# Seven products of a block product summed in three PSUM chains, with partial sums copied out by ScalarE

## The chip, the cores and the metric

The kernel runs on one core of a Trainium2 chip. The metric is the device time of one execution in microseconds (us). A core has five engines, each with its own queue of instructions that it takes in order: TensorE (PE in the profile; its weight loads are PEld), VectorE (DVE), ScalarE (ACT), GpSimd (POOL) and SyncE (SP, which here only issues loads).

## What is computed

A decoder trunk of two layers on 512 tokens of width 1024, in float32. Layer 0 mixes tokens by attention, layer 1 by pooling; each is followed by a SwiGLU FFN of inner width 2816, and every part is preceded by an RMS norm.

```python
def swiglu_ffn(h, w_gate_up, w_down):
    gu = h @ w_gate_up
    gate, up = gu[..., :D_FF], gu[..., D_FF:]
    return (jax.nn.silu(gate) * up) @ w_down

def reference(x, attn_norm, w_qkv, ...):
    for i in range(DEPTH):
        j = i // N_MIXERS
        if i % N_MIXERS == 0:
            x = x + dilated_attention_mixer(rmsnorm(x, attn_norm[j]), w_qkv[j], w_attn_out[j])
        else:
            x = x + pooling_mixer(rmsnorm(x, pool_norm[j]), ...)
        x = x + swiglu_ffn(rmsnorm(x, ffn_norm[i]), w_ffn_gate_up[i], w_ffn_down[i])
    return rmsnorm(x, final_norm)
```

The attention has 8 heads in each of 3 groups; q, k and v of all of them come from one projection `h @ w_qkv`.

## The kernel before

**Split numbers.** Every operand of a large matmul is kept as two float32r tiles, a rounded value `hi` and the rest `lo` (`split`, lines 83 to 85: ScalarE makes `hi`, VectorE subtracts to get `lo`). A product of 128 contraction rows takes three matmuls: hi by hi, hi by lo, lo by hi.

**Block products.** Most of the q, k, v projections and 17 of the 22 column blocks of each FFN's gate and up projection are computed in pairs by the Winograd form of Strassen's scheme: two 128-column outputs (`one` and `two`, for instance gate and up) of 512 tokens from 1024 inputs, cut into quarters of 256 tokens, take seven products instead of eight. Each product (`mult`, lines 378 to 384) has 4 contraction steps by 3 matmuls on 128x256, so a block product has 84 matmuls. There are 55 of them through `seven` (lines 391 to 438): 21 in the attention stage, 34 in the FFN. Four more, for values of the other attention groups, go through `values12`. The first five column blocks of each FFN, the down projections and the pooling stage use plain products of 128x512 (`Product`, lines 262 to 265).

**Operands.** `normed` (lines 440 to 452) makes the sums and differences of token quarters that the scheme needs, and `prepare` (one for the attention, one for each FFN) splits them into the tiles `T["11"]`, `T["21"]`, `T["1"]` to `T["4"]`, `T["22"]`. The weights' sums are made per block product by a `Pair`: `blocks` splits the tile b, `sums` the tile s, `more` adds twice on VectorE (lines 158 and 159) and splits the tile m, `last` splits the half tile l. Products 1 and 2 use b, 5 and 7 use s, 6 and 3 use m, 4 uses l.

**Order of the work.** `seven` issues its products in the order 1, 2, 5, 7, 6, 3, 4, in four PSUM banks (p1, p26, p45, p73). Product 1 is copied out by ScalarE (line 410); VectorE does the other sums as the banks fill: line 423 (2 and 6 with 1), line 429 or 431 (7 and 3 with those), lines 436 and 437 (5 and 4 with those). After each product `behind(i)` calls `pump`, which issues at most one load and one step of the weights to come, as soon as a buffer of its ring is free (`BUFS`: five `w` tiles, two `half`, four `raw`); in the attention stage it also runs functions of the heads (`scores0`, `scores12`, `merge`, `turn0`, `turn12`, `output`), which use all engines. A weight tile is free when the last product that reads it has been issued and done. Loads go by SyncE's queue, and one addition per pair by an accumulating load on GpSimd's (line 145).

The instructions are then put on each engine's queue by the framework in the order in which they are expected to become ready; the written order decides between those that are ready.

In the FFN, `activation` (lines 896 and 897) follows each pair: Silu of the gate on ScalarE, the product with `up` on VectorE, and a split of the result.

Of the kernel before, what the change touches and what calls it, by code (L numbers as in the profile page):

```python
# [11 lines left out]
OP = mybir.AluOpType  # L12
# [43 lines left out]
def trunk(ctx: ExitStack, tc: tile.TileContext, xT, norms, w_first, w_qk, w_qkp, w_v0, w_v0p, w_v12, w_out, w_pair, w_down, w_pin, w_pgrp,  # L56
# [16 lines left out]
    def ps():  # L73
        return psum.tile([P, S], F32, tag="ps", name="ps")
# [8 lines left out]
    def split(hi, lo, v):  # L83
        nc.scalar.activation(hi, v, AF.Copy)  # L84
        nc.vector.tensor_tensor(lo, v, hi.bitcast(F32), op=OP.subtract)  # L85

    rings = {ring: [] for ring in BUFS}

# [286 lines left out]
    def in_place(t, a=slice(0, 2)):  # L375
        return t[:, a.start * H2:a.stop * H2]

    def mult(dst, w, half, T, name):
        for k in range(K2):
            c = slice(half * S + k * P, half * S + (k + 1) * P)  # L380
            th, tl = T[name, k]
            nc.tensor.matmul(dst, w.t[0][:, c], th, start=k == 0, stop=False)  # L382
            nc.tensor.matmul(dst, w.t[0][:, c], tl, start=False, stop=False)  # L383
            nc.tensor.matmul(dst, w.t[1][:, c], th, start=False, stop=k == K2 - 1)  # L384

    def part(unit, name):
        while name not in unit.w:
            pump(must=True)
        return unit.w[name]

    def seven(T, one, two, scratch, after={}, blocks=False):
# [5 lines left out]
        def again(v):  # L397
            return v.unsqueeze(1).to_broadcast([P, 2, H2])

        p1, p26, p45, p73 = ps(), ps(), ps(), ps()  # L400

        def behind(i):
            pump()
            for f in after.get(i, ()):
                f()

        w = part(unit, "b")
        mult(p1[:, :H2], w, 0, T, "11")
        first, sums = scratch("first"), scratch("sums")
        nc.scalar.copy(first[:, :H2], p1[:, :H2])  # L410
        behind(0)
        mult(p26[:, :H2], w, 1, T, "21")
        w.done()
        behind(1)
        w = part(unit, "s")
        mult(p45[:, H2:], w, 0, T, "1")
        behind(2)
        mult(p73[:, :H2], w, 1, T, "3")
        w.done()
        behind(3)  # L420
        w = part(unit, "m")
        mult(p26[:, H2:], w, 0, T, "2")
        nc.vector.tensor_add(into(one), p26, again(first[:, :H2]))
        behind(4)
        mult(p73[:, H2:], w, 1, T, "22")
        w.done()
        if blocks:
            for a in (left, right):
                nc.vector.tensor_add(in_place(sums, a), in_place(p73, a), into(one, right))
        else:  # L430
            nc.vector.tensor_add(sums, p73, again(one[:, H2:]))
        behind(5)
        w = part(unit, "l")
        mult(p45[:, :H2], w, 0, T, "4")
        w.done()
        nc.vector.tensor_sub(into(two), p45, again(sums[:, :H2]))
        nc.vector.tensor_sub(into(one, right), sums[:, H2:], p45[:, H2:])  # L437
        behind(6)

    def normed(layer, k, row):  # L440

        h, t = Held("raw"), Held("raw")
        for i in range(2):
            c = k + i * K2
            nc.vector.scalar_tensor_tensor(h.t[:, i * S:(i + 1) * S], X[c], nrm[:, layer, c:c + 1], row,  # L445
                                           op0=OP.mult, op1=OP.mult)
        hq = h.t.rearrange("p (a b c) -> p a b c", a=2, b=2)
        tq = t.t.rearrange("p (a b c) -> p a b c", a=2, b=2)
        nc.vector.tensor_sub(tq[:, :, 0], hq[:, :, 1], hq[:, 0])
        nc.vector.tensor_sub(t.t[:, H2:S], t.t[:, :H2], h.t[:, 3 * H2:])  # L450
        nc.vector.tensor_add(t.t[:, 3 * H2:], t.t[:, H2:S], h.t[:, S:3 * H2])
        return h, t

    def halves_of(hi, lo):
# [9 lines left out]
    with tc.tile_pool(name="opool", bufs=1) as opool:  # L464
        early = opool.tile([P, HEADS, S], F32R, tag="o", name="early")
        with tc.tile_pool(name="apool", bufs=1) as apool:
# [15 lines left out]
            def values12(after={}):  # L482


                t = apool.tile([P, NT, 4 * P], F32, name="v12")
                unit = units.popleft()

                def product(name, half, key):
                    p = ps()
                    for a in range(2):  # L490
                        for k in range(K2):
                            wh, wl = (v[:, half * S + k % 2 * H2:half * S + (k % 2 + 1) * H2]
                                      for v in part(unit[k // 2], name).t)
# [48 lines left out]
                behind(6)  # L542
                return t

# [177 lines left out]
            def prepare(k):  # L722

                h, t = normed(0, k, rows["row"])
                for i in range(2):
                    held["h", k + i * K2], b = slot("h")
                    H[k + i * K2] = b[:, 0], b[:, 1]
                    split(*H[k + i * K2], h.t[:, i * S:(i + 1) * S])
# [12 lines left out]
                h.done()  # L741
                t.done()
# [141 lines left out]
    with tc.tile_pool(name="fpool", bufs=2) as fpool:  # L884
# [6 lines left out]

        act = []

        def activation(gt, up):

            nc.scalar.activation(gt, gt, AF.Silu)  # L896
            nc.vector.tensor_mul(up, up, gt)
# [17 lines left out]
        def ffn(layer, nxt, lead, row):  # L915
# [23 lines left out]
            def prepare(k):  # L939
# [12 lines left out]
                if k % 2 == 0:  # L952
                    held["t", k, 3], T["n"] = slot("tn", apart=True)
                n = tuple(T["n"][:, e, k % 2 * H2:(k % 2 + 1) * H2] for e in range(2))
                split(*n, b22)
                T["22", k] = n
                h.done()
                t.done()

            def strassen_pair():  # L960
                gt, up = ftile("gt"), ftile("up")
                seven(T, gt, up, ftile)
                activation(gt, up)

            for hf in range(2):
                act.clear()
# [264 lines left out]
```

## Time and profile before

| what | value |
|---|---|
| median of 3 runs | 1218.45 us (1218.39 to 1218.78) |
| the profiled execution | 1219.11 us |
| its span (first to last instruction) | 1217.3 us |
| granted TensorE clock, share of full speed | 0.998 |
| TensorE matmuls busy | 1206.3 us, 9294 of them |
| VectorE busy | 921.7 us |
| ScalarE busy | 574.9 us |
| GpSimd busy | 126.1 us |
| moved from and to HBM | 170.54 MB read, 2.10 MB written |

The profiled execution is one more run beside the three; what lies outside its span is 1.8 us. Busy times are those of the engine, without the issue of loads; the ends of matmuls are modelled, so their starts are the better witnesses. In a group's row stand line, engine, operation, output and inputs by the program's names, shape, count, then busy time and the mean duration of one in ns, then the engine's idle time just before such instructions and what ended it. In a row of the order of time stand start, duration, engine, line and operation, and in brackets the idle time before it and its releaser. A row of waits gives the total, the number and the longest. A row of loads gives count, size and the median time from issue to landing.

### The profile page before, as it was taken

The numbers are of one execution on the slowest core, as the hardware profiler recorded it, in microseconds if no ns is written. First come the engines' busy times: TensorE is split into PE (matmuls) and PEld (weight loads), VectorE is DVE, ScalarE is ACT, GpSimd is POOL, SyncE is SP. The second block draws the span as 40 slices with busy tenths as digits, with TensorE's granted clock in tenths as the row PEclk, the third lists the DMA queues.
The fourth block names the chain that finished last, engine by engine and source line by source line (L and its number), as shares of the span: only waits on it lengthen the run. The fifth ranks groups of instructions, "written<-read, shape, count | busy, mean of one in ns | idle before, by whom it ended". The sixth has DMA issues, their size and how long they took to land.

```text
span 1217.3 us, 22947 instructions
## 1 busy us (share of the span) xinstructions
PE 1206.3 (99%) x9294; PEld 1109.7 (91%) x9294; DVE 921.7 (76%) x1474; ACT 574.9 (47%) x923; POOL 126.1 (10%) x119
## 2 busy tenths in 40 slices
PE   9999999999999999999999999999999999999997
PEld 7889999999999988899889999888789988999987
DVE  6978888978879854889547896659878953798643
ACT  6445555545546553455324554443444632455331
POOL 1111111211111101000001100001301000111000
PEclk9999999999999999999999999999999999999999
DMA  8346567666666632356456774333135645676322
GB/s 280 117 104 171 140 166 170 154 166 156 161 161 149 228 97 92 83 135 176 132 144 170 198 179 121 116 129 121 41 94 127 178 136 137 175 195 183 96 72 70
DMA packets 67306, 174.13 MB, mean 143 GB/s; under 512 B 6896, under 2 KB 8064, under 8 KB 67200
## 3 DMA queue, kind: packets, MB, share of 16 engines
q1 hardware_dynamic: 49248, 137.26, 35.1%
q0 software_dynamic: 17808, 35.14, 17.5%
q8 instruction: 73, 1.20, 0.4%
q14 instruction: 33, 0.27, 0.1%
q10 hardware_dynamic: 144, 0.26, 0.1%
HBM read 170.54 MB, written 2.10 MB: 142 GB/s over the span
## 4 chain that ended last, share of the span: by engine, by line
PE 88%; DVE 8%; issue 2%; DMA 1%; ACT 1%; POOL 0%; SPq 0%; DVEq 0%; POOLq 0%; ACTq 0%
PE ps L382 15%; PE ps L383 14%; PE ps L384 14%; PE ps L262 11%; PE ps L265 11%; PE ps L263 11%; PE ps L496 2%; PE ps L497 2%; PE ps L498 2%; DVE w L85 2%; DVE far L85 1%; PE ps L708 1%; DVE raw L445 1%; PE ps L580 1%; DVE n L315 1%
## 5 line engine op out<-in xcount | busy, mean ns | idle before, releaser
L84 ACT ACTIVATE w<-raw 128x1024 fp32r<-128x1024 f32 (+2 forms) x299 | 298.6, 1005 | 381.6 <-PE ps L265 162.8
L85 DVE TENSOR_TENSOR w<-raw,w 128x1024 fp32r<-128x1024 f32 (+2 forms) x299 | 342.9, 1151 | 140.2 <-ACT w L84 138.2
L383 PE MATMUL ps<-far,w 128*128 128x256 f32 x816 | 224.7, 275 | 0.2
L382 PE MATMUL ps<-far,w 128*128 128x256 f32 x816 | 224.5, 275 | 0.0
L384 PE MATMUL ps<-far,w 128*128 128x256 f32 x816 | 224.5, 275 | 0.0
L383 PEld LDWEIGHTS ps<-far,w 128*128 128x128 f32 x816 | 153.2, 188 | 0.7 <-DVE far L85 0.6
L382 PEld LDWEIGHTS ps<-far,w 128*128 128x128 f32 x816 | 153.2, 188 | 0.2
L384 PEld LDWEIGHTS ps<-far,w 128*128 128x128 f32 x816 | 153.2, 188 | 0.0
L262 PE MATMUL ps<-a,w 128*128 128x512 f32 (+1 forms) x374 | 141.0, 377 | 0.0
L265 PE MATMUL ps<-a,w 128*128 128x512 f32 (+1 forms) x374 | 140.9, 377 | 0.0
L263 PE MATMUL ps<-a,w 128*128 128x512 f32 (+1 forms) x374 | 140.9, 377 | 0.0
L145 POOL DMA_DIRECT2D raw<-w_pair x34 | 41.1, 1209 | 428.5 <-DMA raw<-w_pair 242.1
L265 PEld LDWEIGHTS ps<-a,w 128*128 128x128 f32 x374 | 70.4, 188 | 12.9
L262 PEld LDWEIGHTS ps<-a,w 128*128 128x128 f32 x374 | 70.4, 188 | 12.8
L263 PEld LDWEIGHTS ps<-a,w 128*128 128x128 f32 x374 | 70.4, 188 | 12.8
L382 PE MATMUL ps<-h,w 128*128 128x256 f32 x252 | 71.5, 284 | 0.0
L384 PE MATMUL ps<-h,w 128*128 128x256 f32 x252 | 70.0, 278 | 0.0
L383 PE MATMUL ps<-h,w 128*128 128x256 f32 x252 | 70.0, 278 | 0.0
L896 ACT ACTIVATE gt<-gt 128x512 f32<-128x512 f32 x44 | 27.9, 635 | 47.5 <-DVE gt L437 41.3
L382 PEld LDWEIGHTS ps<-h,w 128*128 128x128 f32 x252 | 47.5, 188 | 0.4
L384 PEld LDWEIGHTS ps<-h,w 128*128 128x128 f32 x252 | 47.4, 188 | 0.0
L383 PEld LDWEIGHTS ps<-h,w 128*128 128x128 f32 x252 | 47.4, 188 | 0.0
(269 smaller groups left out, 2878.6 us busy)
## 6 DMA issues: line engine op xcount, KB each, us to landing
raw<-w_pair SPq DMA_DIRECT2D x78, 512.0 KB, 4.5
raw<-w_qkp SPq DMA_DIRECT2D x36, 512.0 KB, 4.4
raw<-w_pair POOLq DMA_DIRECT2D x34, 512.0 KB, 7.5
raw<-w_down SPq DMA_DIRECT2D x32, 384.0 KB, 3.1
raw<-w_down SPq DMA_DIRECT2D x32, 320.0 KB, 2.9
raw<-w_v SPq DMA_DIRECT2D x18, 512.0 KB, 4.4
raw<-w_qkp POOLq DMA_DIRECT2D x18, 512.0 KB, 7.3
rawhalf<-w_pair SPq DMA_DIRECT2D x34, 256.0 KB, 3.5
```

The costliest lines, as they stand in the source:

```text
L84: nc.scalar.activation(hi, v, AF.Copy)
L85: nc.vector.tensor_tensor(lo, v, hi.bitcast(F32), op=OP.subtract)
L145: nc.gpsimd.dma_start(self.b.t.rearrange("p (a c) -> p a c", a=2), self.src[:, None, 3 * S:].to_broadcast([P, 2, S]), accum_op=OP.add)
L262: nc.tensor.matmul(self.p[:, cols], w[0][:, s], mh[:, cols], start=self.done == 0, stop=False)
L263: nc.tensor.matmul(self.p[:, cols], w[0][:, s], ml[:, cols], start=False, stop=False)
L265: nc.tensor.matmul(self.p[:, cols], w[1][:, s], mh[:, cols], start=False, stop=self.done == self.n)
L382: nc.tensor.matmul(dst, w.t[0][:, c], th, start=k == 0, stop=False)
L383: nc.tensor.matmul(dst, w.t[0][:, c], tl, start=False, stop=False)
L384: nc.tensor.matmul(dst, w.t[1][:, c], th, start=False, stop=k == K2 - 1)
L496: nc.tensor.matmul(o, mh, wh, start=k == 0, stop=False)
L497: nc.tensor.matmul(o, mh, wl, start=False, stop=False)
L896: nc.scalar.activation(gt, gt, AF.Silu)
```

## The change

`seven` issues the products in the order 1, 5, 6, 2, 7, 3, 4. They are summed in three banks: alpha takes products 1, 6, 7 and 4 in turn, each accumulated onto what is there; gamma takes 5 and then 3; beta takes 2. ScalarE copies alpha out after products 1, 6 and 7 and gamma after 5. VectorE makes three quarters of the outputs, each by one operation on 256 elements. The last quarter is alpha with its sign turned: ScalarE writes it, and in the FFN (`inner=True`) the gating product takes it straight from PSUM. For the sums to come out, the operands `T["22"]` and `T["4"]` are prepared with the other sign, and `values12` follows that.

```diff
+    def split_neg(hi, lo, v):
+        nc.scalar.activation(hi, v, AF.Copy, scale=-1.0)
+        nc.vector.scalar_tensor_tensor(lo, v, -1.0, hi.bitcast(F32), op0=OP.mult, op1=OP.subtract)
...
-    def mult(dst, w, half, T, name):
+    def mult(dst, w, half, T, name, on=False):
...
-            nc.tensor.matmul(dst, w.t[0][:, c], th, start=k == 0, stop=False)
+            nc.tensor.matmul(dst, w.t[0][:, c], th, start=k == 0 and not on, stop=False, skip_group_check=on)
...
+        alpha, beta, gamma = (ps()[:, :H2] for i in range(3))
+        ab, cd = scratch("first"), scratch("sums")
+        a, b, c, d = ab[:, :H2], ab[:, H2:], cd[:, :H2], cd[:, H2:]
...
+        wb = part(unit, "b")
+        mult(alpha, wb, 0, T, "11")
+        nc.scalar.copy(a, alpha)
         behind(0)
+        ws = part(unit, "s")
+        mult(gamma, ws, 0, T, "1")
+        nc.scalar.copy(d, gamma)
         behind(1)
+        wm = part(unit, "m")
+        mult(alpha, wm, 0, T, "2", on=True)
+        nc.scalar.copy(b, alpha)
         behind(2)
+        mult(beta, wb, 1, T, "21")
+        wb.done()
+        nc.vector.tensor_add(into(one, left), beta, a)
         behind(3)
+        mult(alpha, ws, 1, T, "3", on=True)
+        ws.done()
+        nc.scalar.copy(c, alpha)
+        nc.vector.tensor_sub(into(two, right), d, c)
         behind(4)
+        mult(gamma, wm, 1, T, "22", on=True)
+        wm.done()
+        nc.vector.tensor_sub(into(one, right), b, gamma)
         behind(5)
         w = part(unit, "l")
+        mult(alpha, w, 0, T, "4", on=True)
         w.done()
+        if not inner:
+            nc.scalar.activation(into(two, left), alpha..., AF.Copy, scale=-1.0)
         behind(6)
+        return alpha
...
 (normed)
-        nc.vector.tensor_add(t.t[:, 3 * H2:], t.t[:, H2:S], h.t[:, S:3 * H2])
+        nc.vector.scalar_tensor_tensor(t.t[:, 3 * H2:], t.t[:, H2:S], -1.0, h.t[:, S:3 * H2], op0=OP.mult, op1=OP.subtract)
...
 (values12)
-                nc.vector.tensor_add(rest, m3, u2)
+                nc.vector.tensor_sub(rest, u2, m3)
...
-                nc.vector.tensor_sub(quarter(0, 1), both(m4), both(u3))
+                nc.vector.scalar_tensor_tensor(quarter(0, 1), both(m4), -1.0, both(u3), op0=OP.mult, op1=OP.subtract)
...
 (activation)
-            nc.vector.tensor_mul(up, up, gt)
+            if left is None:
+                nc.vector.tensor_mul(up, up, gt)
+            else:
+                nc.vector.tensor_mul(up[:, H2:], up[:, H2:], gt[:, H2:])
+                nc.vector.scalar_tensor_tensor(up[:, :H2], left, -1.0, gt[:, :H2], op0=OP.mult, op1=OP.mult)
...
 (prepare of the FFN; that of the attention splits the last quarter alike)
-                split(*n, b22)
+                split_neg(*n, b22)
```

More of the change, by code (lines that the diff above doesn't have):

```diff
@@ L389, in part, with seven @@
         return unit.w[name]
-    def seven(T, one, two, scratch, after={}, blocks=False):
+    def seven(T, one, two, scratch, after={}, blocks=False, inner=False):
         unit, = units.popleft()
         into, left, right = by_block if blocks else in_place, slice(0, 1), slice(1, 2)
-        def again(v):
-            return v.unsqueeze(1).to_broadcast([P, 2, H2])
-        p1, p26, p45, p73 = ps(), ps(), ps(), ps()
+        alpha, beta, gamma = (ps()[:, :H2] for i in range(3))
+        ab, cd = scratch("first"), scratch("sums")
+        a, b, c, d = ab[:, :H2], ab[:, H2:], cd[:, :H2], cd[:, H2:]
         def behind(i):
@@ L405, in behind @@
                 f()
[L407 to L410, printed above, removed]
+        wb = part(unit, "b")
+        mult(alpha, wb, 0, T, "11")
+        nc.scalar.copy(a, alpha)
         behind(0)
-        mult(p26[:, :H2], w, 1, T, "21")
-        w.done()
+        ws = part(unit, "s")
+        mult(gamma, ws, 0, T, "1")
+        nc.scalar.copy(d, gamma)
         behind(1)
-        w = part(unit, "s")
-        mult(p45[:, H2:], w, 0, T, "1")
+        wm = part(unit, "m")
+        mult(alpha, wm, 0, T, "2", on=True)
+        nc.scalar.copy(b, alpha)
         behind(2)
-        mult(p73[:, :H2], w, 1, T, "3")
-        w.done()
+        mult(beta, wb, 1, T, "21")
+        wb.done()
+        nc.vector.tensor_add(into(one, left), beta, a)
         behind(3)
-        w = part(unit, "m")
-        mult(p26[:, H2:], w, 0, T, "2")
-        nc.vector.tensor_add(into(one), p26, again(first[:, :H2]))
+        mult(alpha, ws, 1, T, "3", on=True)
+        ws.done()
+        nc.scalar.copy(c, alpha)
+        nc.vector.tensor_sub(into(two, right), d, c)
         behind(4)
[L425 to L431, printed above, removed]
+        mult(gamma, wm, 1, T, "22", on=True)
+        wm.done()
+        nc.vector.tensor_sub(into(one, right), b, gamma)
         behind(5)
         w = part(unit, "l")
-        mult(p45[:, :H2], w, 0, T, "4")
+        mult(alpha, w, 0, T, "4", on=True)
         w.done()
-        nc.vector.tensor_sub(into(two), p45, again(sums[:, :H2]))
-        nc.vector.tensor_sub(into(one, right), sums[:, H2:], p45[:, H2:])
+        if not inner:
+            nc.scalar.activation(into(two, left), alpha.rearrange("p (y x z) -> p y x z", y=Y16 // 2, z=2) if blocks else alpha,
+                                 AF.Copy, scale=-1.0)
         behind(6)
+        return alpha
     def normed(layer, k, row):
@@ L727, in prepare @@
                     H[k + i * K2] = b[:, 0], b[:, 1]
-                    split(*H[k + i * K2], h.t[:, i * S:(i + 1) * S])
+                    b = H[k + i * K2]
+                    if i:
+                        split(*(v[:, :H2] for v in b), h.t[:, S:3 * H2])
+                        split_neg(*(v[:, H2:] for v in b), h.t[:, 3 * H2:])
+                    else:
+                        split(*b, h.t[:, :S])
                 T["11", k] = halves_of(*H[k])[0]
@@ L961, in strassen_pair @@
                 gt, up = ftile("gt"), ftile("up")
-                seven(T, gt, up, ftile)
-                activation(gt, up)
+                activation(gt, up, seven(T, gt, up, ftile, inner=True))
             for hf in range(2):
```

7 lines of the change are left out of this document (4 added, 3 removed).

## The prediction

> **What bounds the kernel now.** I read the page first, then stretches of busy time, then the order of time on three engines inside one block product of the FFN.
>
> ```profile
> ## 1 busy us (share of the span) xinstructions
> PE 1206.3 (99%) x9294; PEld 1109.7 (91%) x9294; DVE 921.7 (76%) x1474; ACT 574.9 (47%) x923; POOL 126.1 (10%) x119
> ```
>
> ```profile
> 140.00:440.00 300.00, 300.00 (x3110) 295.87 (x3109) 244.50 (x439) 158.09 (x311) 43.20 (x44) 1.00 0.63 163
> 691.90:701.42 9.52, 9.52 (x87) 9.52 (x85) 8.71 (x13) 5.49 (x8) 1.20 (x1) 1.00 0.73 193
> 895.00:925.00 30.00, 30.00 (x136) 24.89 (x135) 29.09 (x47) 15.66 (x25) 1.20 (x1) 1.00 0.22 53
> ```
>
> The columns are the stretch, its length, busy time of TensorE, its weight loads, VectorE, ScalarE, GpSimd, the granted clock and the DMA share. The first is the attention stage, the second one FFN block product, the third the FFN's plain products with the operands being prepared. TensorE is busy throughout, but the ends of matmuls are modelled, so this has to be checked against their starts:
>
> ```profile
> 692.13 0.28 PE L384 MATMUL ps<-far,half 128*128 128x256 f32 x1
> 692.24 0.28 PE L382 MATMUL ps<-far,w 128*128 128x256 f32 x1
> ...
> 694.96 0.28 PE L382 MATMUL ps<-far,w 128*128 128x256 f32 x1
> ```
>
> ```profile
> 691.13 1.07 ACT L84 ACTIVATE w<-raw 128x1024 fp32r<-128x1024 f32 x1 [1.71 <-PE ps L384]
> 692.44 0.64 ACT L84 ACTIVATE half<-rawhalf 128x512 fp32r<-128x512 f32 x1 [0.24 <-PE ps L384]
> 693.85 0.37 ACT L410 COPY first<-ps 128x256 f32<-128x256 f32 x1 [0.78 <-PE ps L384]
> 694.58 0.64 ACT L896 ACTIVATE gt<-gt 128x512 f32<-128x512 f32 x1 [0.35 <-DVE gt L437]
> 695.24 1.07 ACT L84 ACTIVATE w<-raw 128x1024 fp32r<-128x1024 f32 x1
> 696.38 0.64 ACT L84 ACTIVATE a<-up 128x512 fp32r<-128x512 f32 x1
> 697.88 1.07 ACT L84 ACTIVATE w<-raw 128x1024 fp32r<-128x1024 f32 x1 [0.86 <-PE ps L384]
> 700.65 1.07 ACT L84 ACTIVATE w<-raw 128x1024 fp32r<-128x1024 f32 x1 [1.70 <-PE ps L384]
> ```
>
> From 692.24 to 694.96 lie 24 matmuls (two of the seven products), one each 0.113 us. The weight split at 691.13 returns at 700.65, so a block product lasts 9.52 us, and 84 matmuls by 0.113 are 9.5. There TensorE never waits, and no relief of VectorE (8.71 of 9.52 busy) can shorten it. What the change can still do is put a wait where there is none.
>
> ```profile
> 691.20 0.68 DVE L158 TENSOR_TENSOR raw<-raw 128x512 f32<-128x512 f32 x1
> 691.80 0.68 DVE L431 TENSOR_TENSOR sums<-ps,gt 128x512 f32<-128x512 f32 x1
> 692.40 1.21 DVE L85 TENSOR_TENSOR w<-raw,w 128x1024 fp32r<-128x1024 f32 x1
> 693.53 0.68 DVE L436 TENSOR_TENSOR up<-ps,sums 128x512 f32<-128x512 f32 x1
> 694.13 0.41 DVE L437 TENSOR_TENSOR gt<-sums,ps 128x256 f32<-128x256 f32 x1
> 694.46 0.69 DVE L159 TENSOR_TENSOR raw<-raw 128x512 f32<-128x512 f32 x1
> ```
>
> Lines 158 and 159 stand next to each other in the source, yet four instructions of other steps lie between them: a queue holds its instructions in the order in which they were expected to become ready, not in the written order. That decides most of what follows.
>
> **The change part by part.** First the work. An FFN block product loses on VectorE three operations on 512 elements (0.68 each), one on 256 (0.41) and the gating product on 512 (0.69 by its like on 512), 3.14 us; it gains three on 256 and a gating product halved into one of 256 and one fused of 256 (0.41 each, the fused one some 0.48 by the row of L1098 below): 2.1 us. VectorE falls by 1.0 to 7.7 us of 9.52. ScalarE gains three copies of 0.37: 6.6 of 9.52. In the 21 products of the attention stage it also writes the negated last quarter. TensorE keeps its 84 matmuls.
>
> Then the waits. I count products by their place in the new order. The first, third, fifth and seventh (numbers 1, 6, 7, 4) sum in one bank, alpha; the second and sixth (5, 3) in gamma; the fourth (2) has beta alone. The third may not start before ScalarE's copy of alpha after the first has read it; so with the fifth and seventh after the third and fifth, and with the sixth, which has four products' time. Take 0 as the first matmul. A product takes 1.36 us, and its last matmul ends 0.17 after the next one's first start (692.13 + 0.28 = 692.41 against 692.24). So the seven ends are at 1.53, 2.89, 4.25, 5.61, 6.97, 8.33 and 9.69. The copy at 693.85 started 0.08 after its product ended (693.77). One other product lies between, so alpha's next one is due 1.19 us after that end; of these, 0.08, 0.37 for the copy and about 0.04 for the signal are spent, and **0.70 us is the slack**: a copy that ScalarE takes up at most that late costs nothing. A split takes 1.07, and a copy that has just missed its turn costs 1.07 - 0.70 = 0.37 us.
>
> [...]
>
> Now one FFN unit on ScalarE. Weight buffers come free later than before: product 1's and 21's tile (b) after the fourth product instead of the second, the tile s after the fifth instead of the fourth, m after the sixth as before. So ScalarE does: m's split of the next unit 5.65 to 6.72; the copy after the fifth product, 7.05 to 7.42; b's split to 8.49; s's to 9.56; the Silu to 10.20; the small split to 10.84; the first copy of the next unit, ready at 11.13, to 11.50, and its limit is 9.52 + 2.72 - 0.41 = 11.83. The split of the activations follows VectorE's fused product and ends at 12.57; the copy after the second product (12.57 to 12.94) isn't needed until the sixth at 16.3; the one after the third comes at 13.85 on an idle engine. Each tight copy keeps its full 0.70 and 0.3 us of idle time before it. Cost: nothing, as long as the queue has this order.
>
> Weights and loads: the next m is complete on VectorE at 7.9 and due at 12.24 (its product is now the third, not the fifth): 4.3 us to spare. Its raw tile is released there too, against 5.3 now (the split that began at 695.24 ends 4.1 after 692.24, and VectorE's subtraction takes 1.2), so SyncE's reload starts 2.6 later, at 8.0:
>
> ```profile
> raw<-w_pair SPq DMA_DIRECT2D x78, 512.0 KB, 4.5
> ```
>
> It lands at 12.5 and is split at 9.52 + 6.97 = 16.5. The accumulating load on GpSimd's queue needs only the other raw tile, whose last reader stays at s's split, so it does not move. Loads cost nothing; were that cover of 4 us gone, each microsecond of delay would reach ScalarE's next split and the copy behind it.
>
> The preparation gets fused negations for plain ones, 24 on 256 elements in all, 16 in the FFN:
>
> ```profile
> L451 DVE TENSOR_TENSOR raw<-raw 128x256 f32<-128x256 f32 x12 | 5.1, 421 | 0.1
> ...
> L1098 DVE SCALAR_TENSOR_TENSOR x<-x,nrm,ps 128x256 f32<-128x256 f32 x8 | 3.3, 477 | 0.4 <-PE ps L345 0.4
> ```
>
> 0.056 us each, 0.45 per FFN layer, 0.9 in both. TensorE covers it, but in 895:925 VectorE is busy 29.09 of 30.00, so the cover is thin: between 0 and 0.9 I take 0.5. The eight of the attention operands, four more on 512 in the value blocks and four splits cut in two lie where VectorE has 55 us of 300 left; nothing.
>
> The attention stage has the same slack but more on ScalarE:
>
> ```profile
> L410 ACT COPY first<-ps 128x256 f32<-128x256 f32 x55 | 20.2, 367 | 25.6 <-PE ps L384 25.6
> ```
>
> ```profile
> ACT first L410 <- PE ps L384: 25.6, 35, 0.8
> ```
>
> ```profile
> 242.60 0.35 ACT L410 COPY first<-ps 128x256 f32<-128x256 f32 x1
> ```
>
> ```profile
> 239.63 0.28 PE L382 MATMUL ps<-h,w 128*128 128x256 f32 x1
> ...
> 242.35 0.28 PE L382 MATMUL ps<-t,w 128*128 128x256 f32 x1
> ```
>
> Of 55 first copies ScalarE stood waiting for 35; in the other 20 it was at other work. The one at 242.60 stood behind four exponentials; its product began at 239.63, so alpha would be due at 242.35 and TensorE would wait until 242.98: 0.63 us. Bounds: 0, because the fourth product (bank beta) needs no copy and can be queued ahead, to 20 x 0.63 = 12.6 us. I take 0.5, since the queues follow readiness, as lines 158 and 159 show.
>
> **Sum.** 0 + 0.5 + 0.5 = 1.0 us. The profiled execution took 1219.11 us (span 1217.3), 0.66 above the median of 1218.45; on that median the forecast is 1219.5, in its own case 1217 to 1220.8.
>
> **The rivals.**
> *Late copies in the attention stage (slower).* TensorE's queue keeps the written order and half of the bound comes true: 6.5 us, 1225. For it: the row at 242.60. Against it: the readiness order.
>
> *A copy behind a split in every FFN unit (slower).* At 6.97 the copy after the fifth product and b's split become ready together, because one matmul releases both. If the split goes first, the copy ends 0.08 + 1.07 + 0.37 + 0.04 after the end, 0.37 too late; 34 FFN units (17 of 22 columns in two layers) make 12.6 us, 1231. It decides whenever a split of over 0.70 stands ahead. Worse, the first copy could stand behind the activations' split, which waits for VectorE:
>
> ```profile
> ACT a L84 <- DVE up L897: 20.7, 19, 3.2
> ```
>
> Nineteen such waits average 1.1 us. In my layout this copy would end at 12.94 with the next product due at 12.24: 0.7 a unit, 24 us, 1242. Against both: the written order puts the copy first, and the split of activations isn't ready in time to overtake it. [...]
>
> *Relief of VectorE (faster).* In places of the attention stage matmuls start 0.118 apart:
>
> ```profile
> 215.02 0.28 PE L382 MATMUL ps<-h,w 128*128 128x256 f32 x1
> ...
> 216.44 0.28 PE L382 MATMUL ps<-h,w 128*128 128x256 f32 x1
> ```
>
> Twelve matmuls in 1.42 us. If that came from VectorE's traffic, 21 x 84 x 0.005 = 8.8 us is the most to be had; a third, 3 us, gives 1215.5. Against it: at 239.63 products run at 0.113 in the same stage, with the same load on VectorE by the stage's row.
>
> *The change does not do what it says* in the sense that VectorE's saving buys nothing: that is the forecast itself.
>
> **How the numbers follow.** Forecast 0.43. Late copies in attention 0.26: the coupling is new, and its slack is shorter than a split. FFN copies behind a split 0.15. Relief 0.16. About 0.2% (2.4 us) is what a measurement of this kernel can tell from no change, so same has the forecast's 0.43, faster 0.16, slower 0.26 + 0.15 = 0.41. The range runs from 1215.0 (the relief case at its value) to 1232.0 (one copy a unit behind a split); what is left out is the 1242 case and a larger relief, under 0.2 together. The forecast's own 1217 to 1220.8 stands beside it.
>
> **What would show it.** Right: a block product of the FFN again returns after 9.5 us, VectorE's busy time falls by some 60 us (34 x 1.0, and 21 x 1.2 where no gating product is halved), ScalarE's rises by some 70 us (55 x 3 x 0.37 is 61, and 21 last quarters), copies start 0.1 after their product, the chain stays on TensorE. Late copies: starts of TensorE's third, fifth or seventh product in 140:440 over 0.3 us after the matmul before, with a wait for ScalarE. FFN misplacement: the return takes 9.9 us or more. Relief: the 0.118 spacing gone. Wrong altogether: a stage without block products that has changed by over 1 us, or TensorE waiting for weights of the third product.

## The result and the profile after

The changed kernel takes 1248.98 us (median of four runs, 1246.22 to 1253.24), the kernel before 1218.51 beside it (1218.39 to 1218.78). The ratio is 1.0253 with a 95% interval of 1.0217 to 1.0289: 30 us slower, above the range of 1215.0 to 1232.0. The profiled execution took 1246.22 us, the quickest of the four, with a span of 1244.4 against 1217.3.

The page after has the span, the busy times and the engines of the chain that ended last:

```profile
span 1244.4 us, 23001 instructions
PE 1217.0 (98%) x9294; PEld 1118.0 (90%) x9294; DVE 866.1 (70%) x1448; ACT 631.2 (51%) x1113; POOL 121.7 (10%) x119
PE 80%; DVE 10%; issue 3%; DMA 3%; ACT 3%; POOL 0%; POOLq 0%; DVEq 0%; ACTq 0%; SPq 0%
```

VectorE fell by 55.6 us and ScalarE rose by 56.3. TensorE has the same 9,294 matmuls, but is busy for 10.7 us more: some of them run more slowly (starts 0.21 us apart instead of 0.113, as the rows below show). The chain, which lay on TensorE for 88% before, now spends 3% on DMA and 3% on ScalarE, where it spent 1% on each.

A long steady stretch of FFN block products comes first, because the forecast rested on it. The view of stretches for the kernel after, and then for the kernel before (same columns as in the prediction, 230 us each):

```profile
600.00:830.00 230.00, 230.00 (x1502) 209.37 (x1501) 142.64 (x228) 108.08 (x163) 13.27 (x11) 1.00 0.54 147
```

```profile
590.00:820.00 230.00, 230.00 (x1478) 208.34 (x1476) 152.85 (x227) 97.87 (x128) 13.27 (x11) 1.00 0.54 148
```

TensorE is busy all the time in both. ScalarE in order of time, one block product after:

```profile
715.69 0.64 ACT L84 ACTIVATE a<-up 128x512 fp32r<-128x512 f32 x1 [0.86 <-DVE up L910]
716.22 0.36 ACT L416 COPY sums<-ps 128x256 f32<-128x256 f32 x1
...
723.97 0.38 ACT L412 COPY first<-ps 128x256 f32<-128x256 f32 x1 [0.26 <-PE ps L388]
725.20 0.64 ACT L84 ACTIVATE a<-up 128x512 fp32r<-128x512 f32 x1 [0.85 <-DVE up L910]
```

The split of the activations returns after 725.20 - 715.69 = 9.51 us, as it did before. (The copies after the first, second, third and fifth product are now lines 412, 416, 420 and 428; the three matmuls are lines 386 to 388; line 84 is still the high half of a split.) In the steady state the change costs nothing.

Where the time goes is found by counting TensorE's matmuls. Both traces have the same number, so the start of the nth matmul after, less its start before, is the delay gathered by then:

| start in the kernel before, us | delay, us |
|---|---|
| 185 | 0.7 |
| 192 | 5.0 |
| 285 | 6.0 |
| 297 | 8.6 |
| 385 | 9.7 |
| 395 | 12.0 |
| 539 | 12.4 |
| 543 | 20.6 |
| 930 | 20.4 |
| 937 | 20.7 |
| 940 | 27.2 |
| 1210 | 27.2 |

The delay grows in five steps of 4.3, 2.5, 2.3, 8.1 and 6.5 us, together 23.7 of 27.2, and hardly at all between them. Three lie in the attention stage, at the last block product ahead of the value blocks of heads 3, 5 and 7; two in the FFN, at the second block product of each layer. The view of waits names what TensorE, and then ScalarE, waited for (total us, times, longest):

```profile
PE ps L386 <- ACT first L412: 17.5, 8, 5.3
...
ACT w L84 <- DMA raw<-w_v: 12.1, 5, 4.7
...
ACT w L84 <- DMA raw<-w_pair: 11.2, 2, 5.9
```

Eight waits for the first copy, five of them long; the other three are of 0.55 us, behind four exponentials and no load. At the second long one of the attention stage the view of waits names TensorE for the split (4.29 us of idle time, so it is not in the rows above), but the chain of waits shows a load of w_v there too, landing at 294.11, 0.09 us before the split starts. Here is the longest in TensorE's order of time, kernel after:

```profile
550.81 0.28 PE L388 MATMUL ps<-far,w 128*128 128x256 f32 x1
550.92 0.28 PE L386 MATMUL ps<-far,w 128*128 128x256 f32 x1
...
552.17 0.28 PE L388 MATMUL ps<-far,w 128*128 128x256 f32 x1
557.72 0.58 PE L386 MATMUL ps<-far,w 128*128 128x256 f32 x1 [5.27 <-ACT first L412]
558.09 0.41 PE L387 MATMUL ps<-far,w 128*128 128x256 f32 x1
558.31 0.41 PE L388 MATMUL ps<-far,w 128*128 128x256 f32 x1
```

The first product ends with the matmul at 550.81, the second with that at 552.17. The third, which adds onto alpha, starts 5.55 us later. After it the matmuls start 0.21 apart instead of 0.113. ScalarE over the same time:

```profile
548.36 1.06 ACT L84 ACTIVATE w<-raw 128x1024 fp32r<-128x1024 f32 x1
555.31 1.06 ACT L84 ACTIVATE w<-raw 128x1024 fp32r<-128x1024 f32 x1 [5.89 <-DMA raw<-w_pair]
556.27 0.61 ACT L905 ACTIVATE gt<-gt 128x512 f32<-128x512 f32 x1
556.79 0.61 ACT L84 ACTIVATE half<-rawhalf 128x512 fp32r<-128x512 f32 x1
557.31 0.35 ACT L412 COPY first<-ps 128x256 f32<-128x256 f32 x1
```

ScalarE did nothing for 5.89 us. At the head of its queue stood a weight split whose load had not landed, and the copy that TensorE needed stood three places behind it. The copy could have started 0.08 after 551.09, the end of the first product. It started 6.14 late; less the slack of 0.70 that is 5.44, and TensorE's gap is 5.55 less the usual 0.11, 5.44. The same reckoning gives the other seven waits of this trace to 0.02 us.

Why the load was late is in the chain of waits (start, length, what):

```profile
541.09 0.44 DVE raw L455
...
541.58 4.14 DMA raw<-w_pair
...
546.29 8.86 DMA raw<-w_pair
...
555.31 0.10 ACT w L84
...
557.41 0.27 ACT first L412
...
557.72 0.58 PE ps L386
```

The FFN's operands are prepared in the same ring of four raw tiles that the weights are loaded into. VectorE's last addition there (line 455) frees a tile at 541.53; only then can SyncE load, and behind that GpSimd's accumulating load, which took 8.86 us.

The view of stretches shows the second half of the price, in the column of the granted clock (the seventh entry after the stretch, ahead of the last two):

```profile
545.00:552.40 7.40, 7.40 (x63) 7.13 (x61) 5.30 (x8) 3.28 (x5) 1.58 (x2) 1.00 0.74 197
552.40:557.70 5.30, 0.04 (x1) 0.00 (x0) 1.30 (x2) 2.39 (x5) 0.82 (x1) 0.88 0.96 210
557.70:563.20 5.50, 5.49 (x25) 5.49 (x26) 3.00 (x6) 1.24 (x3) 0.00 (x0) 0.50 0.49 152
```

After the wait the clock was 0.50 for the 5.5 us in which TensorE worked again, which loses half of that, 2.75 us. With the wait's 5.44 that is 8.2; the step in the table is 8.1. The step at 937 is a wait of 4.82 and 3.4 us at half clock, 6.5 in all; the step at 185 a wait of 2.54 and 3.4 us at half clock, 4.2. The two other steps had waits of 2.2 us and no loss of clock.

The attention stage shows the same figure on ScalarE, with a load of w_v and the exponentials ahead of the copy:

```profile
186.86 1.06 ACT L84 ACTIVATE w<-raw 128x1024 fp32r<-128x1024 f32 x1 [4.68 <-DMA raw<-w_v]
187.82 0.36 ACT L439 ACTIVATE qk<-ps 128x256 f32<-128x256 f32 x1
188.09 0.42 ACT L593 ACTIVATE s<-s,nm 128x160 f32<-128x160 f32 x1
...
189.74 0.35 ACT L412 COPY first<-ps 128x256 f32<-128x256 f32 x1
```

The loads were late before as well. The kernel before, ScalarE's order of time at the same place of the FFN, and TensorE's stretch around it:

```profile
541.04 1.07 ACT L84 ACTIVATE w<-raw 128x1024 fp32r<-128x1024 f32 x1 [3.66 <-DMA raw<-w_pair]
...
542.53 0.35 ACT L410 COPY first<-ps 128x256 f32<-128x256 f32 x1
```

```profile
535.00:545.00 10.00, 10.00 (x91) 10.00 (x90) 6.50 (x10) 4.01 (x6) 1.42 (x2) 1.00 0.89 202
```

There too ScalarE stood 3.66 us for w_pair with the first copy behind the split. But TensorE, with columns of its own for every product, asked for nothing of the copy and ran through (busy for 10.00 of the 10.00 us). The theory to test follows: the late load is old; new is that TensorE waits for whoever waits for it.

### The profile page after: what moved, and what is told of

The parts are those of the page before. It is cut to its first block, busy times and chain, and to the rows that moved or that the text cites. A ratio compares the mean times of both kernels' runs of the same rounds, so it can differ in the third digit from the quotient of the medians.

```text
span 1244.4 us, 23001 instructions
## 1 busy us (share of the span) xinstructions
PE 1217.0 (98%) x9294; PEld 1118.0 (90%) x9294; DVE 866.1 (70%) x1448; ACT 631.2 (51%) x1113; POOL 121.7 (10%) x119
## 4 chain that ended last, share of the span: by engine, by line
PE 80%; DVE 10%; issue 3%; DMA 3%; ACT 3%; POOL 0%; POOLq 0%; DVEq 0%; ACTq 0%; SPq 0%
PE ps L386 12%; PE ps L387 12%; PE ps L388 12%; PE ps L266 11%; PE ps L267 11%; PE ps L269 11%; DVE w L85 2%; PE ps L500 2%; DMA raw<-w_pair 2%; PE ps L502 2%; PE ps L501 2%; PE ps L712 1%; DMA raw<-w_v 1%; ACT w L84 1%; DVE far L85 1%
## 5 line engine op out<-in xcount | busy, mean ns | idle before, releaser
L386 PEld LDWEIGHTS ps<-far,w 128*128 128x128 f32 x816 | 154.8, 190 | 10.5 <-ACT first L412 10.3
L387 PEld LDWEIGHTS ps<-far,w 128*128 128x128 f32 x816 | 155.1, 190 | 0.7 <-DVE far L85 0.6
L388 PEld LDWEIGHTS ps<-far,w 128*128 128x128 f32 x816 | 154.9, 190 | 0.0
L424 DVE TENSOR_TENSOR gt<-ps,first 128x256 f32<-128x256 f32 x34 | 14.4, 425 | 46.2 <-PE ps L388 46.2
```

What stands on the lines that cost most here:

```text
L386: nc.tensor.matmul(dst, w.t[0][:, c], th, start=k == 0 and not on, stop=False, skip_group_check=on)
```

## The experiments

**Theory**: TensorE's third product hangs on ScalarE's queue, and at the five transitions a split that waits for its load stands ahead of the copy there. **Rivals**: the new product order makes weights late; ScalarE simply has too much work; the added sign turns and last quarters delay something.

**The wait taken away.** Products 1, 6 and 7 get banks of their own; order, copies and VectorE's sums stay.

```diff
-        alpha, beta, gamma = (ps()[:, :H2] for i in range(3))
+        a1, a6, a7, alpha, beta, gamma = (ps()[:, :H2] for i in range(6))
...
-        mult(alpha, wm, 0, T, "2", on=True)
-        nc.scalar.copy(b, alpha)
+        mult(a6, wm, 0, T, "2")
+        nc.scalar.copy(b, a6)
```

> The changed kernel with a bank of its own for each of the products 1, 6, 7 and 4: nothing is accumulated across products (the sums across products are left out), the copies by ScalarE, the product order, the releases and the loads stay as they are, but no product waits for a copy. Theory: 1217 to 1222, no wait of TensorE for ScalarE over 0.5 us, the half-clock stretches gone, although the same split still waits for its load as long as before. Both rivals (ScalarE's added work, late weight releases): 1240 or more.

1224.11 us (1221.44 to 1224.67), ratio 1.0042 (1.0028 to 1.0056). ScalarE's order of time and TensorE's waits:

```profile
541.67 1.06 ACT L84 ACTIVATE w<-raw 128x1024 fp32r<-128x1024 f32 x1 [4.88 <-DMA raw<-w_pair]
...
543.68 0.35 ACT L412 COPY first<-ps 128x256 f32<-128x256 f32 x1
```

```profile
PE ps L386 <- ACT sums L416: 1.6, 4, 0.5
```

The split still waits 4.88 us and the copy starts some 5 us after it could, but TensorE no longer cares: no gap over 0.75 us (start to start) is left in the block products, and 25 of the 30 us are gone. Not every sum across products is left out: the sixth product still adds onto gamma, and the four waits in the row are for gamma's copy. The median lies somewhat above what was expected. The relief of VectorE is all there, and it buys nothing.

**The order alone.** The banks, signs and sums of before, in the order 1, 5, 6, 2, 7, 3, 4.

```diff
-        mult(p1[:, :H2], w, 0, T, "11")
-        mult(p26[:, :H2], w, 1, T, "21")
-        mult(p45[:, H2:], w, 0, T, "1")
+        mult(p1[:, :H2], wb, 0, T, "11")
+        mult(p45[:, H2:], ws, 0, T, "1")
+        mult(p26[:, H2:], wm, 0, T, "2")
+        mult(p26[:, :H2], wb, 1, T, "21")
...
```

> The kernel before with the new product order 1, 5, 6, 2, 7, 3, 4 alone, its four banks and VectorE's sums kept. Theory: 1217.5 to 1221, since no product waits for a copy. Rival two (late releases of weight tiles): 1240 or more, with TensorE waiting for VectorE's subtractions at the third product. Rival one says 1218 too.

1221.52 (1220.93 to 1222.97), ratio 1.0025 (1.0014 to 1.0036). The waits of TensorE's weight loads:

```profile
PEld ps L384 <- DVE w L85: 2.1, 6, 0.8
```

The rival is real but small: the weights m are wanted two products earlier, and at the two FFN transitions TensorE waits for VectorE's half of their split. The longest are at 549.7 and 948.2. By count of matmuls the delay of this trace grows by 1.3 us from 543 to 575 and by 1.6 us from 937 to 1000, which is all of its 2.9 us. Three of the thirty.

**One stage at a time.** The new form in the FFN alone, with the old function and signs in the attention stage; and the other way round.

```diff
-                        seven(T, QKV[h, g, 0], QKV[h, g, 1], scratch, between(h, g), g == 0)
+                        seven_old(T, QKV[h, g, 0], QKV[h, g, 1], scratch, between(h, g), g == 0)
```

> The change in the 34 block products of the FFN alone; the 21 of the attention stage and the value blocks as before. By the account of added gaps in the two traces (FFN 15.5 us, half of it two waits of 5.4 and 4.8 us and the half clock after them): 1231 to 1237 us. A theory in which every block product pays alike gives 34/55 of 30 us, 1237; one in which the attention stage alone pays, 1219.

> The change in the 21 block products of the attention stage and the value blocks alone; the FFN as before. By the account of added gaps (12.1 us, of them three waits of 2.3 to 2.7 us and three of 0.55): 1228 to 1234 us. If every block product paid alike: 1230; so the verdict is in the trace: three gaps of over 2 us before the third product of the block product that precedes the value blocks, none elsewhere over 0.7.

FFN alone: 1233.21 (1232.19 to 1234.33), ratio 1.0118 (1.0103 to 1.0133). Attention alone: 1232.82 (1232.09 to 1233.37), ratio 1.0114 (1.0097 to 1.0131). TensorE's waits, FFN alone first:

```profile
PE ps L386 <- ACT first L461: 9.2, 2, 4.8
```

```profile
PE ps L386 <- ACT first L461: 8.7, 6, 3.4
```

The two cost 14.3 and 14.0 us, together 28.3 of 30.5: they add up, and each has its own waits. Two waits in the FFN (start to start 4.68 and 5.03), three long and three of 0.66 in the attention stage. Both came as expected.

**Without the accumulating load.** This tests the lateness itself, on the kernel after and on the one before.

```diff
-            nc.gpsimd.dma_start(self.b.t.rearrange("p (a c) -> p a c", a=2),
-                                self.src[:, None, 3 * S:].to_broadcast([P, 2, S]), accum_op=OP.add)
```

> The changed kernel without the accumulating load of each weight pair (it leaves out one of the two summands of the tile that s and m are made of), so that this tile has landed some 9 us earlier. Theory (a weight split that waits for a late load stands at the head of ScalarE's queue, the copies behind it make TensorE wait, and the long waits lower the granted clock): the five waits of 2.3 to 5.5 us and the half-clock stretches after them go, 1219 to 1226 us. Rival one (the copies are simply too much for ScalarE, or VectorE is late): nothing changes, 1245 to 1253. Rival two (weight tiles are released later in the new product order and their splits come late): nothing changes either, 1240 or more.

> The kernel before without the accumulating load (one summand of the weight sums left out), as the base line for e1_no_accumulate. Theory: there TensorE waits for no copy, so the load is worth nothing: 1216.5 to 1219.5. If the load cost TensorE time by itself, it would be 1212 or less, and the gain of e1_no_accumulate would be no evidence for the waits.

After: 1228.36 (1227.94 to 1228.99), ratio to the kernel before 1.0079 (1.0064 to 1.0094). Before, without it: 1218.70 (1218.05 to 1219.37), ratio 0.9999 (0.9990 to 1.0008). The waits of TensorE in the first (line numbers are two lower there):

```profile
PE ps L384 <- ACT first L410: 5.0, 6, 1.7
```

The same load is worth 20 us to the kernel after and nothing to the one before. The FFN's two long waits are gone, and so is the half clock before the last microseconds. In the attention stage 1.98, 1.24 and 1.42 remain, where the late load is the plain one of w_v; that was not reckoned with, and the time lies 2 us above the expected stretch.

**A fifth raw tile.** This makes the loads early in another way, without leaving anything out.

```diff
-BUFS = {"w": 5, "half": 2, "raw": 4, "rawhalf": 2}
+BUFS = {"w": 5, "half": 2, "raw": 5, "rawhalf": 2}
...
-SLOTS = 15
+SLOTS = 14
```

> The changed kernel with five raw tiles for loaded weights in place of four (one of the FFN's 15 spare operand slots makes room), so that a load need not wait for a tile that VectorE still reads and goes out some us earlier; all else, the copies too, as in the change. Theory (the waits are the lateness of loads, passed on through ScalarE's queue): the FFN's waits of 5 us shrink to under 2.5 and those of the attention stage shrink too, 1222 to 1236 us. If lateness is set by the DMA engines and not by the free tile, 1244 to 1253.

> The kernel before with five raw tiles and one operand slot less, the base line for the run above. Theory: TensorE waits for no copy there, so earlier loads are worth nothing: 1217.5 to 1220 us. If it falls below 1216, part of the other run's gain is not the waits.

After with five: 1228.32 (1227.15 to 1229.46), ratio 1.0084 (1.0067 to 1.0101). Before with five: 1221.66 (1220.25 to 1222.30), ratio 1.0023 (1.0013 to 1.0034). TensorE's waits, after with five and then before with five:

```profile
PE ps L386 <- ACT first L412: 2.7, 6, 0.5
```

```profile
PE ps L553 <- DVE vt L474: 2.0, 1, 2.0
```

The five long waits are gone, those of the FFN altogether. The other sizes cost the kernel before 3 us, which was not expected: all of it comes at one place, the wait in the second row at 55 us, with 3.4 us at half clock after it. The kernel after with five has a like wait there, in its profile without the half clock, so a microsecond or two of what follows is uncertain. Against that base line the change costs 6.7 us instead of 30. So the ring of four raw tiles sets the lateness, and the lateness sets most of the price.

**The copies on VectorE.** If ScalarE's queue is the obstacle, another engine's queue should free them, at the price of its own work.

```diff
-        nc.scalar.copy(a, alpha)
+        nc.vector.tensor_copy(a, alpha)
...
```

> The changed kernel with the four copies of partial sums made by VectorE in place of ScalarE. Theory: at the long waits VectorE too stood with the subtraction that follows the late split at the head of its queue (5.5 us at 556), so the copies get no further: the five long waits stay, 1235 to 1255. Rival one (ScalarE has too much to do): 1217 to 1223.

1247.24 (1245.74 to 1249.55), ratio 1.0235 (1.0220 to 1.0251). TensorE's waits, and then those of its weight loads:

```profile
PE ps L386 <- DVE first L412: 6.5, 6, 1.9
```

```profile
PEld ps L386 <- DVE sums L428: 6.4, 23, 0.6
```

The long waits shrank to 1.77, 1.33, 0.89, 1.49 and 2.21; it had been expected that they stay. In their place came many short ones, in the steady FFN too: from 660 to 740 us of the kernel before the delay grows by 3.5 us, where it did not grow with ScalarE's copies. There a subtraction of 1.22 us stands ahead of a copy with 0.70 us of slack (at 686.44, the copy at 687.58, and TensorE's next product starts 0.35 us after the matmul before). The same total by another mixture, so the time alone would have told nothing.

**The splits queued behind the copy.** The splits of the weights are put behind the copy after the third product by hand.

```diff
-        nc.scalar.copy(b, alpha)
-        behind(2)
+        behind(2, nc.scalar.copy(b, alpha))
...
-            pump()
+            if copied:
+                with tc.issue_after(copied.ins):
+                    pump(3)
+            else:
+                pump(1 if i in (3, 4) else 0)
```

> The changed kernel with the same instructions and loads, but the splits of the next pair's tiles b and s are put on ScalarE's queue behind the copy after the third product of a later block product, where before they went in after the fifth to seventh product and stood ahead of that product's first copy when their load was late. Theory (a split that waits for its load at the head of ScalarE's queue): the two waits of 5 us in the FFN and most of the three of 2.3 to 2.7 us in the attention stage go, 1221 to 1231 us. If the added copies as such cost the time, or the late load must be paid anyway, it stays at 1243 or more.

1234.73 (1233.89 to 1235.57), ratio 1.0130 (1.0115 to 1.0145). The waits of TensorE's weight loads:

```profile
PEld ps L388 <- ACT first L418: 6.3, 26, 0.9
```

No gap of TensorE over 1.12 us (start to start) is left in this trace. Here is ScalarE at the FFN's second block product, where the longest wait was:

```profile
546.71 0.38 ACT L418 COPY first<-ps 128x256 f32<-128x256 f32 x1 [0.18 <-PE ps L390]
...
549.37 0.37 ACT L426 COPY first<-ps 128x256 f32<-128x256 f32 x1 [0.93 <-PE ps L390]
549.64 2.01 ACT L84 ACTIVATE w<-raw 128x1024 fp32r<-128x1024 f32 x2
```

The accumulating load was as late as ever: it landed at 550.55, 3.9 us after the first product's end, against 4.1 in the kernel after. But the copy no longer stood behind the split. So the order of the queue was what made the long waits out of the late loads. An order that is right at the transitions is wrong in the steady state, though: 26 short waits, and 2.6 us of delay from 660 to 740. The time lies above the expected stretch.

**The new form only where loads are early?** The FFN's first two block products keep the old sums (with the new signs), first with the old attention stage, then with the new one, where the last block product ahead of the values of odd heads is old too.

```diff
-                activation(gt, up, seven(T, gt, up, ftile, inner=True))
+                if early:
+                    seven_neg(T, gt, up, ftile)
+                    activation(gt, up)
+                else:
+                    activation(gt, up, seven(T, gt, up, ftile, inner=True))
...
+                        strassen_pair(j < NPLAIN + 2)
```

> The change in the FFN alone and there from the third block product of each layer on; the first two of each layer sum as before. Theory (steady block products cost nothing; the two layers each pay one wait in the second block product and the half clock after it): 1218.5 to 1221 us against 1233 with all 34. If a copy in every block product costs something, 32 of 36 parts stay: 1231 to 1233. If the wait only moves to the next block product, a wait of 2 us or more shows some 20 us after the first block product.

> The whole change, but the first two block products of each FFN layer and the last one before the value blocks (g = 2 of each odd head) sum as before: 48 of 55 block products keep the three chains. Theory: the five long waits and the half clock go, the three of 0.55 us after the heads' outputs and small ones stay: 1221 to 1226 us. If the cost is spread over the block products: 48/55 of 30 us, 1244.

1226.76 (1226.18 to 1227.35), ratio 1.0066 (1.0051 to 1.0081), and 1231.31 (1229.35 to 1235.11), ratio 1.0108 (1.0086 to 1.0130). In the FFN of both, TensorE's wait moved on by one block product, to the first one with the new form, and became shorter (2.45 and 2.52 us in the first kernel, start to start); for the first kernel that had been named as the third outcome. TensorE's waits in the first kernel, and its ScalarE there:

```profile
PE ps L386 <- ACT first L461: 4.4, 2, 2.2
```

```profile
547.41 2.95 ACT L84 ACTIVATE w<-raw 128x1024 fp32r<-128x1024 f32 x3
550.27 0.61 ACT L84 ACTIVATE half<-rawhalf 128x512 fp32r<-128x512 f32 x1
550.79 0.35 ACT L461 COPY first<-ps 128x256 f32<-128x256 f32 x1
```

Here no load is awaited any more. The splits that the late loads held up stand together, three in 2.95 us, and the copy behind them. So in the FFN lateness hands itself on for at least one block product: leaving out the first two takes the price from 14.3 to 8.2 us, not to nothing. In the attention stage, where the value blocks with a bank for each product come next, the second kernel has no long wait left, and the delay at 480 us is 4.6 us instead of 12.0. Both times lie above what was expected.

**The same kernel again**, one more execution.

> The changed kernel once more, for a second profile. The same five waits at the same places, to 0.1 us. What may differ is which of them is followed by a half-clock stretch: after those over 4 us always, after the three of 2.3 to 2.7 us by chance; each such stretch of 3.4 us costs up to 1.7 us, which would account for runs from 1246 to 1253.

1251.55 us, with waits (start to start) of 4.22, 4.58, 2.22, 4.31 and 5.48 where the first profile had 2.65, 2.26, 2.30, 5.55 and 4.93. They were expected to agree within 0.1. The lengths follow when a load lands, which differs from run to run: counted from the end of the first product, the split ahead of the copy starts 1.57 and 2.32 us later than in the first profile at the first two places, 1.23 earlier at the fourth and 0.55 later at the fifth, and each wait changed by just that. With one more stretch at half clock (1.7 us) this is 4.8 of the 5.3 us between the two executions, and it fits the spread of 7 us over the four runs. The kernel before, with the same loads and nobody on TensorE waiting for them, spreads by 0.4 us beside it and by 1.9 at most in the other rounds.

## Why the prediction was wrong

The steps that held:
- An FFN block product costs nothing in the steady state: 9.51 us, copies 0.1 after their product or soon enough, the activations' split where the layout put it.
- The slack of 0.70 us: with it the longest wait comes out to within 0.01 us, and the others to 0.02.
- VectorE fell by 55.6 us (some 60 forecast), ScalarE rose by 56.3 (some 70).
- The preparation: from 395 to 539 the delay went from 12.0 to 12.4 us, from 830 to 937 from 20.6 to 20.7; 0.5 was put down for both layers.
- No stage without block products changed by over 1 us. That exclusion was right, and the delays are all at block products.

The step that failed is "It lands at 12.5 and is split at 9.52 + 6.97 = 16.5", and with it "Loads cost nothing". It was worked out for one block product in the middle of the FFN and then taken for all. There the cover of 4 us is real. At the second block product of each layer the loads stand behind a ring of raw tiles that the preparation has filled, and ahead of the values of heads 3, 5 and 7 behind one that weights have filled (the value blocks take two pairs at once, which is all four tiles). There is no cover at all in these places. The prediction named the price of that case, "each microsecond of delay would reach ScalarE's next split and the copy behind it", and that is what happened. It did not ask whether the case occurs, though the trace of the kernel before shows it among ScalarE's waits for DMA: the 3.66 us at 541.04, with the first copy behind it. The term set at 0 measured some 14 us in the FFN alone.

The second mis-sized term is the attention stage, 0.5 forecast and 14.0 measured. The reason given for taking so little, that queues follow readiness, is true of the expected readiness. A load that landed later than was expected when the order was written didn't change the order here: ScalarE stood 4.68 us ahead of the split at 186.86, and the copy kept its place behind that split and the exponentials (189.74). The rival for this stage (6.5 us; half of its bound of 12.6 is 6.3) had the right engine and the right waiting product, and its sign came true: six third products start 0.66 to 2.65 us after the matmul before, with a wait for ScalarE. It thought of exponentials in ten products. Exponentials alone cost 0.55 us in three; in three others it was a late load, with exponentials behind it.

The rival with a copy behind a split had the right mechanism, in the wrong place and at the wrong price: not 0.37 us in each of 34 units, but 5 us in two, because the split stood still. The copy that could have started at 551.17 started at 557.31, with a waiting split ahead of it and ScalarE idle for 4.14 us of that time (551.17 to 555.31).

Two smaller misses. The order alone costs 2.7 us, where 4.3 us to spare had been worked out for the weights m; that figure too belongs to the steady state. And a wait of TensorE was priced at its length, but the half clock after it can cost more than half of it again (2.54 us made 4.2). The relief of VectorE, the faster rival, is excluded for this kernel: with it and without the long waits the time is still 1.0042 of before, and the twelve matmuls that took 1.41 us from 215.02 before take 1.41 us from 219.99 after, so the 0.118 spacing did not go with VectorE's work.

What stays open: of the last 3.5 us of the delay (27.2 less the five steps) the three waits of 0.55 in the attention stage are known, and the rest, in pieces of under 0.5, was not taken apart. None of these versions beats the kernel before.

## What to carry to other kernels

In these runs a PSUM bank that was accumulated onto after another engine had copied it out tied TensorE to that engine's whole queue, and so to a load that a split ahead of the copy waited for: at 557.72 TensorE had stood 5.27 us for a copy of 0.35, ahead of which a split had waited 5.89. Before such a change, list in the trace of before where the copying engine waits for DMA, above all at the passages between stages where buffers are shared, and ask who will wait for it then: a wait that cost nothing (3.66 us in the kernel before) is the price list of the change. Work the layout out at the worst unit as well as at the steady one, and look for the delay in the units that follow too: with the FFN's first two block products summed as before it moved on by one block product and was still 2.45 and 2.52 us there.

## What the hardware showed

A short stop of TensorE also slowed what followed. In the first profile of the kernel after, the granted clock is 0.50 in three stretches at such stops: 3.41 us from 191.16 after a wait (start to start) of 2.65, 6.83 us from 556.38 at the wait of 5.55, and 3.41 us from 962.57 at the wait of 4.93; at the waits of 2.26 and 2.30 it stays at 1.00. In the half-clock stretches matmuls of 256 columns start 0.21 us apart instead of 0.113. In the other runs waits of 2.94, 3.68 and 4.2 us or more were all followed by 0.50 for about 3.4 or 6.8 us too; none of 2.26 us or less was. Between them it differed: 2.27 us, 2.0 of them idle, brought it (the kernel before with five raw tiles, at 55 us), and so did 2.45, but 2.52 did not in the same trace as the 2.45, nor did 2.30, 2.33 and 2.44 in others. Why, these runs do not show.

The accumulating load took 8.86 us from issue to landing at the passage into the FFN, against 4.14 for the plain load ahead of it. That the same kernel's time could vary by 7 us, most of it by the landing of loads as far as two profiles show, had not been expected either.
